# The queues of four engines tied to the order of the source, in a decoder block on one core

## The chip, the cores and the metric

The kernel runs on one core of one Trainium2 chip. The metric is the device time of one execution, in microseconds (us), as the median of several executions; less is better. The engines are named as the profile names them: PE (TensorE, matmuls and transposes; PEld are its weight loads), DVE (VectorE), ACT (ScalarE), POOL (GpSimd) and SP (SyncE, which issues most DMAs). Each engine works through a queue of its own, in the order in which the program was written out for it; between engines, semaphores hold an instruction back until what it reads or overwrites is ready.

## The reference

One layer of a decoder: a gated short convolution and stick-breaking attention run on the same normalised input, are merged by sigmoid gates and projected; then a gated MLP with a causal convolution between its up-projection and its gelu. 1024 tokens and 16 meta tokens, width 1024, 16 heads of 64, MLP width 2816, all in fp32:

```python
h = xn @ w_in
b_c, c_c, h_c, q, k, v, g_conv, g_attn = jnp.split(h, list(splits), axis=-1)
y_conv = b_c * causal_dwconv(c_c * h_c, conv_w_mix)
branch_conv = y_conv @ w_proj_conv
...
z = jnp.einsum("bqhd,bkhd->bhqk", qb, kb) * scale
log_beta = jax.nn.log_sigmoid(z)
log_fail = jnp.where(causal, log_beta - z, 0.0)
survive = lax.cumsum(log_fail, axis=3, reverse=True) - log_fail
a = jnp.where(causal, jnp.exp(log_beta + survive), 0.0)
...
merged = sigmoid(g_conv + b_gate[0]) * branch_conv + sigmoid(g_attn + b_gate[1]) * branch_attn
mixed = merged @ w_out
...
u, g = jnp.split(xn @ w_up_gate, 2, axis=-1)
u = causal_dwconv(u, conv_w_ffn)
return (jax.nn.gelu(u) * g) @ w_down
```

Around both parts stand RMS norms before and after, and the residual is added.

## The kernel before

**Precision.** Each fp32 operand of a matmul is split into a high and a low part (`split`, L64): ACT casts the high one (L65), and DVE or POOL subtracts it from the source for the low one (L66). A product then takes three matmuls: high by high, high by low, low by high.

**Stages**, by the clock of the profile:

- 0 to 80: inputs, norms, the transposed input xnT, and the first operands.
- 80 to 410: 14 *early pairs*, two column blocks of `w_in` each, for the convolution (c, h, b) and for gates. A pair is done by one level of Strassen's scheme (`strassen`): seven products in place of eight, for each of two halves of the tokens (260 columns). The seven operands S1, S2, A12 and so on are sums of blocks of the raw weights, made one step at a time by the generator `weight_ops` for the pair that comes next, into a ring of eight slots; the steps are called between the products. In each half, ACT copies the first three banks into `snap_e` (L600, L603, L606); later products add onto the same banks, so they wait for these copies. `done_ch` puts the convolution's steps on a list `todo`, whose entries are run one after each product: POOL's product c * h (L640), ACT's scaling (L643), DVE's two multiply-adds (L645 to L647).
- 410 to 1025: attention for eight pairs of heads, a period of about 70 us each. `stage1` makes the scores z on PE, ACT a sigmoid `fl` (L359), DVE a scan over it (L366). `stage2` transposes the scanned blocks (L394, PE), ACT casts the high part `ah` (L398), DVE makes the low part `al` (L401), PE multiplies both by the values (L384, L385), and ACT and DVE move the result out (L421, L422). In between run matmuls of the q, k and v projections (L138 to L140), with their evacuations `qh`, `ql` (L237, L238, L232), `kk` (L252, L256) and `vv` (L287, L288).
- 1025 to 1260: gates and the two branch projections. Rows that were written to DRAM are loaded again and split (`yT`, `oT`); gates leave PSUM through ACT (L332).
- 1260 to 1420: the out-projection by blocks of tokens, each with a norm (`post_block`, L1026 to L1059, which ends in the normalised `xv` and its transpose), and the first operands of the FFN (`op_split`, `x_t1` and so on).
- 1420 to 1833: the FFN's up-projection, 22 pairs of column blocks by the same Strassen scheme. Even pairs make u, in two halves of 258 and 256 columns; odd pairs make the gate, 512 columns wide. `products` (L1149 and after) has three copies into `snap` (L1169, L1172, L1175) at the same places, and `prep_pair` makes the operands of the next pair, a step after each product (a gate pair) or after every second one (a u pair), into a ring of eight slots. Between a u pair and its gate pair stands `conv_gelu` (L1333): for each of two blocks the convolution (`conv3`: ACT L204, DVE L205 and L206) and the Gelu (ACT L1337).
- 1833 to 2086: the down-projection, the last norm and the output.

**What sets the order.** The source writes the work out in one sequence, with generators that interleave the stages by hand. The framework then schedules it: in each engine's queue an instruction may be placed ahead of one that the source has earlier, where the framework's own estimate has it ready first. The order in the source is thus a wish, and the program's order the scheduler's. Of the instructions behind the first 80 us, 833 of PE's 12566 stand elsewhere than in the source (by at most 39 places), 1011 of DVE's 1691 (by up to 88), and on ACT and POOL 307 and 77 neighbours stand the other way round. The queue of SP and the DMAs are scheduled in the same way.

The loop of the FFN, for the place of `conv_gelu`:

```python
        if gate:
            conv_gelu(p)
            sets = [products(i, 1, 512, bank, evac_g(p))]
...
        for si, st in enumerate(sets):
            for k, _ in enumerate(st):
                if gate or (7 * si + k) % 2:
                    next(prep, None)
```

Of the kernel before, what the change touches and what calls it, by code (L numbers as in the profile page):

```python
# [33 lines left out]
def block_kernel(ctx, tc, x, meta_tokens, g_pre_mix, w_in, channels, w_proj_conv,  # L34
                 w_proj_attn, w_out, g_post_mix, g_pre_ffn, w_up_gate, w_down,
                 g_post_ffn, out):
    nc = tc.nc
# [409 lines left out]
    dense = Dense(ps_mm0, items)  # L447
# [94 lines left out]
    for i in range(2):  # L542
        next(tops_gen)
        start_chunk(i, 9)
    dense.i, dense.total = 2, 48

    RING1 = ["ap", "ap", "ap", "ap", "wlo", "whi", "wlo", "whi"]
    ring1_at = [2]
# [182 lines left out]
    for i in range(len(early_pairs)):  # L731
        last = i + 1 == len(early_pairs)
# [104 lines left out]
                cur, credit = cur + 1, 0.0  # L837


    at_ctx.close()  # L840
    slots_abc = ctx.enter_context(ExitStack())
    slotA = slots_abc.enter_context(pool("slotA", 1, "right"))
# [584 lines left out]
    for gi, fbs in enumerate(groups):  # L1427
        last = gi == len(groups) - 1
# [13 lines left out]
        for tb in range(8):  # L1442
# [23 lines left out]
            if last:  # L1466
# [3 lines left out]
                for hf in range(2):  # L1470
# [2 lines left out]
                                                   op0=ALU.mult, op1=ALU.add)  # L1473
                    (nc.sync if hf else nc.scalar).dma_start(out[tb * P:(tb + 1) * P, c], a[:, c])


# [1 line left out]
_OUTS = [((1024, 1024), "float32")]  # L1478
# [53 lines left out]
```

## Time and profile before

| | |
|---|---|
| median of 3 executions | 2082.77 us (2081.93 to 2088.43) |
| the profiled execution | 2088.08 us, of which its span 2086.3 us |
| PE clock granted, mean | 0.981 of full speed |
| instructions | 31469 |
| largest groups by busy time | matmuls L138, L139, L140 (291.5, 280.3, 279.9 us) and the FFN's L1160, L1162, L1164 (171.1, 169.0, 168.8 us) |
| DVE's largest group | the scans L366, 195.7 us |

The stage table in the prediction has, for each stretch of the span, the busy microseconds of each engine with the number of instructions, then the granted clock of PE as a share of full speed, the busy share of the DMA engines, and GB/s. A row of a timeline is: start, duration, engine, line, operation, output and inputs with their shapes; a bracket behind it has the idle time of that engine just before and what ended it. A row of the waits is: the engine and what waited, what it waited for, and then the sum, the count and the longest one, in us.

### The profile page before, as it was taken

The page shows a single profiled execution, that of the slowest core. Times are in us where ns is not written, and L with a number is a line of the kernel's source. Part 1 is how long each engine was busy: PE and PEld are TensorE (multiplying, and loading weights), DVE is VectorE, ACT ScalarE, POOL GpSimd, SP SyncE. Part 2 cuts the span into 40 slices and gives each one's busy share as a digit, 9 for nine tenths or more (in the row PEclk, how much of TensorE's full clock was granted, in tenths as well). Part 3 has the DMA queues.
Part 4 walks back from the last instruction along what each step waited for, and adds up shares of the span by engine and source line. Part 5 has one row for each costly group of instructions (what it writes and reads, how often), then busy time and mean ns, then how long its engine had stood idle before and what let it go on. Part 6 is the DMA issues. An engine that isn't in the chain of part 4 may idle for free.

```text
span 2086.3 us, 31469 instructions
## 1 busy us (share of the span) xinstructions
PE 1970.3 (94%) x12564; PEld 1842.9 (88%) x12564; DVE 1109.3 (53%) x1689; ACT 838.7 (40%) x1709; POOL 815.9 (39%) x644
## 2 busy tenths in 40 slices
PE   6889999999999999999999989979999999999997
PEld 6889999998999899889999989978899899878886
DVE  6733443247777777776342114785444444445546
ACT  6433333435555555555441212354334434412122
POOL 2644544422221222122122561225656555555353
PEclk9999999999999999999999999999999999999999
DMA  3212221310100010002374574313222121253323
GB/s 133 87 55 62 70 67 47 109 44 21 41 31 21 31 41 31 21 31 61 85 239 172 168 201 129 101 56 101 71 92 81 61 102 67 76 182 101 101 81 131
DMA packets 56175, 177.60 MB, mean 85 GB/s; under 512 B 12872, under 2 KB 12872, under 8 KB 56028
## 3 DMA queue, kind: packets, MB, share of 16 engines
q1 hardware_dynamic: 52704, 165.09, 24.7%
q10 hardware_dynamic: 3324, 10.50, 1.6%
q8 instruction: 98, 1.61, 0.3%
q14 instruction: 49, 0.40, 0.1%
HBM read 131.36 MB, written 44.21 MB: 84 GB/s over the span
## 4 chain that ended last, share of the span: by engine, by line
PE 36%; DMA 6%; DVE 5%; POOL 3%; ACT 2%; issue 1%; ACTq 0%; SPq 0%; DVEq 0%; POOLq 0%
PE st L1160 6%; PE st L1164 5%; PE st L1162 5%; PE st L1454 3%; PE st L1452 3%; PE st L1453 3%; PE mm L138 2%; PE mm L139 2%; PE mm L140 2%; POOL a_op L66 1%; DMA raw<-in_w_up_gate_dram 1%; DMA ld<-y_d 1%; DVE xr L69 1%; PE po L1007 1%; PE po L1009 1%
## 5 line engine op out<-in xcount | busy, mean ns | idle before, releaser
L122 POOL TENSOR_TENSOR wlo<-raw,whi 128x256 fp32r<-128x256 f32 x208 | 172.4, 859 | 331.0 <-ACT whi L119 307.1
L138 PE MATMUL mm<-xnT,whi 128*128 128x342 f32 (+1 forms) x864 | 291.5, 338 | 7.7 <-ACT gt L332 3.6
L140 PE MATMUL mm<-xnT,wlo 128*128 128x342 f32 (+1 forms) x864 | 279.9, 324 | 3.6 <-POOL wlo L122 3.6
L139 PE MATMUL mm<-xnT,whi 128*128 128x342 f32 (+1 forms) x864 | 280.3, 324 | 0.1
L66 POOL TENSOR_TENSOR a_op<-raw,a_op 128x512 fp32r<-128x512 f32 (+1 forms) x136 | 191.9, 1425 | 91.6 <-ACT a_op L65 87.3
L366 DVE TENSOR_TENSOR_SCAN fl<-fl,upper 114x128 f32<-114x128 f32 (+2 forms) x144 | 195.7, 1379 | 28.2 <-ACT fl L359 26.9
L69 DVE TENSOR_TENSOR raw<-raw 128x512 f32<-128x512 f32 x72 | 72.1, 1001 | 210.3 <-POOL a_op L66 106.3
L1160 PE MATMUL st<-opT,a_op 128*128 128x258 f32 (+2 forms) x528 | 171.1, 324 | 6.6 <-ACT snap L1175 3.8
L138 PEld LDWEIGHTS mm<-xnT,whi 128*128 128x128 f32 x864 | 165.6, 192 | 11.7 <-ACT gt L332 4.2
L1162 PE MATMUL st<-opT,a_op 128*128 128x258 f32 (+2 forms) x528 | 169.0, 320 | 1.3 <-DVE v L76 0.9
L140 PEld LDWEIGHTS mm<-xnT,wlo 128*128 128x128 f32 x864 | 165.3, 191 | 4.2 <-POOL wlo L122 4.2
L1164 PE MATMUL st<-opT,a_op 128*128 128x258 f32 (+2 forms) x528 | 168.8, 320 | 0.0
L139 PEld LDWEIGHTS mm<-xnT,whi 128*128 128x128 f32 x864 | 165.8, 192 | 1.8 <-DVE xnT L66 0.7
L590 PE MATMUL st<-tT,s_op 128*128 128x260 f32 x448 | 130.3, 291 | 20.6 <-ACT snap_e L600 16.3
L65 ACT CAST a_op<-raw 128x512 fp32r<-128x512 f32 (+1 forms) x136 | 85.1, 634 | 159.8 <-DMA raw<-in_w_up_gate_dram 56.6
L1459 DVE TENSOR_TENSOR acc<-acc,st 128x512 f32<-128x512 f32 x144 | 98.4, 687 | 91.1 <-PE st L1454 91.1
L398 ACT CAST ah<-tp 114x342 fp32r<-114x342 f32 (+3 forms) x288 | 109.0, 400 | 91.9 <-PE tp L394 87.2
L401 DVE TENSOR_TENSOR al<-tp,ah 114x342 fp32r<-114x342 f32 (+3 forms) x288 | 118.1, 449 | 35.1 <-ACT ah L398 32.6
L66 POOL TENSOR_TENSOR s_op<-raw,s_op 128x512 fp32r<-128x512 f32 x84 | 119.6, 1437 | 40.9 <-ACT s_op L65 30.2
L359 ACT ACTIVATE fl<-z 114x348 f32<-114x348 f32 (+10 forms) x240 | 109.9, 464 | 61.4 <-PE z L358 60.8
L594 PE MATMUL st<-tT,s_op 128*128 128x260 f32 x448 | 129.0, 288 | 0.0
L592 PE MATMUL st<-tT,s_op 128*128 128x260 f32 x448 | 129.0, 288 | 0.0
(200 smaller groups left out, 5556.9 us busy)
## 6 DMA issues: line engine op xcount, KB each, us to landing
raw<-in_w_in_dram SPq DMA_DIRECT2D x64, 512.0 KB, 3.4
raw<-in_w_up_gate_dram SPq DMA_DIRECT2D x44, 512.0 KB, 3.5
act_d<-owork SPq DMA_DIRECT2D x22, 512.0 KB, 4.3
araw<-act_d SPq DMA_DIRECT2D x22, 512.0 KB
raw<-in_w_down_dram SPq DMA_DIRECT2D x22, 512.0 KB, 3.2
y_d<-su SPq DMA_DIRECT2D x8, 513.0 KB
o_d<-ot SPq DMA_DIRECT2D x8, 513.0 KB
ld<-y_d SPq DMA_DIRECT2D x8, 513.0 KB, 5.2
```

The lines of the kernel that those rows point to most:

```text
L66: (lo_engine or nc.vector).tensor_tensor(lo, src, hi.bitcast(F32), op=ALU.subtract)
L122: nc.gpsimd.tensor_tensor(lo[:, c], raw[:, c], hi[:, c].bitcast(F32), op=ALU.subtract)
L138: nc.tensor.matmul(ps, wh, xh, start=(kb == 0), stop=False)
L139: nc.tensor.matmul(ps, wh, xl, start=False, stop=False)
L140: nc.tensor.matmul(ps, wl, xh, start=False, stop=(kb == KB - 1))
L366: nc.vector.tensor_tensor_scan(fl[:, ::-1], fl[:, ::-1], upper[:, NT - nk:][:, ::-1], 1.0, op0=ALU.mult, op1=ALU.max)
L590: nc.tensor.matmul(ps, wt[:, 0, k], xh, start=start and kb == 0, stop=False, skip_group_check=True)
L592: nc.tensor.matmul(ps, wt[:, 0, k], xl, start=False, stop=False, skip_group_check=True)
L594: nc.tensor.matmul(ps, wt[:, 1, k], xh, start=False, stop=stop and kb == 3, skip_group_check=True)
L1160: nc.tensor.matmul(ps, wt[:, 0, k], xh, start=start and kb == 0, stop=False, skip_group_check=True)
L1162: nc.tensor.matmul(ps, wt[:, 0, k], xl, start=False, stop=False, skip_group_check=True)
L1164: nc.tensor.matmul(ps, wt[:, 1, k], xh, start=False, stop=stop and kb == 3, skip_group_check=True)
```

## The change

Two edits. Before the attention stage's buffers are given back, a generator of weight operands (`dense`) is run on by one step. And at the end of the program a function walks over all instructions that came after the preamble, in the order of the source, and ties each one of PE, ACT, DVE and POOL, other than DMA issues, to the one before it on the same engine. These ties make no semaphore wait; they only keep the scheduler from putting a later instruction first. SP and the DMAs are left free.

```diff
@@ -543,6 +543,7 @@
         start_chunk(i, 9)
     dense.i, dense.total = 2, 48
+    first = len(nc.cur_bb.bb.instructions)
 
@@ -837,6 +838,8 @@
+    if dense.gen is not None:
+        dense.until(dense.i + 1)
     at_ctx.close()
@@ -1473,6 +1476,22 @@
+    in_program_order(tc, nc, first)
+
+
+def in_program_order(tc, nc, first, engines=("PE", "Activation", "DVE", "Pool")):
+    last = {}
+    for ins in list(nc.cur_bb.bb.instructions)[first:]:
+        name = ins.engine.name
+        if name not in engines or "DMA" in type(ins).__name__.upper():
+            continue
+        if name in last:
+            tc.add_manual_dep(ins, last[name].name,
+                              mybir.DependencyInfo(mybir.DependencyClass.NoSync,
+                                                   mybir.DependencyReason.DATA),
+                              reason="program order")
+        last[name] = ins
```

Lines behind L546 move down by one, those behind L840 by three: L600 becomes L601, L1169 becomes L1172, L1337 becomes L1340.

**ACT around a gate pair of the FFN.** The rows of the program before, from the end of a u pair on (a_op and raw are operands of the next pair, owork the convolution's tiles, st a bank, snap its copy):

```order
L204 ACTIVATE owork<-owork,par_ffn 128x1024
L1213 COPY owork<-st 128x255
L204 ACTIVATE owork<-owork,par_ffn 128x1024
L65 CAST a_op<-raw 128x512
L1169 COPY snap<-st 128x512
L1337 ACTIVATE owork<-owork 128x1024
L65 CAST a_op<-tmp_s 128x512
L1172 COPY snap<-st 128x512
L1337 ACTIVATE owork<-owork 128x1024
```

The same place after the change:

```order
L1216 COPY owork<-st 128x255
L65 CAST a_op<-raw 128x512
L204 ACTIVATE owork<-owork,par_ffn 128x1024
L1340 ACTIVATE owork<-owork 128x1024
L204 ACTIVATE owork<-owork,par_ffn 128x1024
L1340 ACTIVATE owork<-owork 128x1024
L1172 COPY snap<-st 128x512
L65 CAST a_op<-raw 128x512
```

The first bank's copy stood between the second L204 and the first Gelu, and now stands behind both Gelus; the second L204 now stands behind the first Gelu.

**ACT around a pair of the early stage** that follows on a finished c and h (s_op are operands of the next pair; su the tiles of the result). Before:

```order
L704 COPY su_1139<-st_1246 128x260
L643 ACTIVATE su_1138<-su_919,par_66 128x1026
L643 ACTIVATE su_1139<-su_920,par_66 128x1026
L600 COPY snap_e_592<-st_1359 128x260
L65 CAST s_op_1388<-raw_1353 128x512
L603 COPY snap_e_592<-st_1360 128x260
L606 COPY snap_e_592<-st_1359 128x260
L704 COPY su_1358<-st_1359 128x260
L65 CAST s_op_1420<-tmp_e_591 128x512
L600 COPY snap_e_592<-st_1468 128x260
L65 CAST s_op_1451<-raw_1353 128x512
```

After:

```order
L601 COPY snap_e_592<-st_1359 128x260
L604 COPY snap_e_592<-st_1360 128x260
L65 CAST s_op_1388<-raw_1353 128x512
L607 COPY snap_e_592<-st_1359 128x260
L65 CAST s_op_1420<-tmp_e_591 128x512
L65 CAST s_op_1451<-raw_1353 128x512
L644 ACTIVATE su_1138<-su_919,par_66 128x1026
L705 COPY su_1358<-st_1359 128x260
L601 COPY snap_e_592<-st_1468 128x260
L65 CAST s_op_1483<-raw_1353 128x512
L644 ACTIVATE su_1139<-su_920,par_66 128x1026
L604 COPY snap_e_592<-st_1469 128x260
```

The two scalings (L643, then L644) stood ahead of the pair's first snap and now stand behind the three of its first half; the casts of S1 and S2 (s_op_1420 and s_op_1451) stood around the first snap of the second half (from st_1468), and now both stand ahead of it.

**DVE in the attention stage**, at the block of scans near 630 us (fl are scanned, qh and ql evacuate the q projection, al is the low part that PE waits for). Before:

```order
L366 SCALAR_TENSOR_TENSOR fl_6406<-fl_6406,upper_4035 114x242
L366 SCALAR_TENSOR_TENSOR fl_6415<-fl_6415,upper_4035 114x356
L366 SCALAR_TENSOR_TENSOR fl_6424<-fl_6424,upper_4035 114x470
L366 SCALAR_TENSOR_TENSOR fl_6433<-fl_6433,upper_4035 114x584
L366 SCALAR_TENSOR_TENSOR fl_6449<-fl_6449,upper_4035 114x698
L238 CAST qh_6273<-mm_6394 64x342
L401 TENSOR_TENSOR al_6490<-tp_6485,ah_6489 128x342
L401 TENSOR_TENSOR al_6501<-tp_6496,ah_6500 114x342
L238 CAST qh_6274<-mm_6394 64x342
L232 TENSOR_TENSOR ql_6275<-mm_6394,qh_6273 64x342
```

After:

```order
L366 SCALAR_TENSOR_TENSOR fl_6264<-fl_6264,upper_4035 114x1040
L366 SCALAR_TENSOR_TENSOR fl_6400<-fl_6400,upper_4035 114x128
L366 SCALAR_TENSOR_TENSOR fl_6406<-fl_6406,upper_4035 114x242
L366 SCALAR_TENSOR_TENSOR fl_6415<-fl_6415,upper_4035 114x356
L366 SCALAR_TENSOR_TENSOR fl_6424<-fl_6424,upper_4035 114x470
L366 SCALAR_TENSOR_TENSOR fl_6433<-fl_6433,upper_4035 114x584
L238 CAST qh_6273<-mm_6394 64x342
L238 CAST qh_6274<-mm_6394 64x342
L232 TENSOR_TENSOR ql_6275<-mm_6394,qh_6273 64x342
L232 TENSOR_TENSOR ql_6276<-mm_6394,qh_6274 64x342
L422 TENSOR_TENSOR ot_6237<-av_6311,ot_6237 64x342
L401 TENSOR_TENSOR al_6490<-tp_6485,ah_6489 128x342
```

The scan of 1040 columns stood some dozen rows higher and is now at the head of the block; both qh and both ql now stand ahead of the first al, and the scan of 698 (fl_6449) behind the row shown last.

## The prediction

> **What bounds the kernel now.** I read the page first, then the busy times by stage, then what TensorE (PE) waited for, and then the stretches in which the order of a queue decides.
>
> ```profile
> PE 1970.3 (94%) x12564; PEld 1842.9 (88%) x12564; DVE 1109.3 (53%) x1689; ACT 838.7 (40%) x1709; POOL 815.9 (39%) x644
> ```
>
> PE is busy for 94% of the span of 2086.3 us: 116 us of the whole program are without a matmul, so an order that only removes waits can't gain more than that and the time at half clock. An order that makes PE wait has no such limit. The stages:
>
> ```profile
> core 0: us, PE busy (x) PEld busy (x) DVE busy (x) ACT busy (x) POOL busy (x), PEclk, DMA share, GB/s
> ...
> 410.00:1025.00 615.00, 587.09 (x3918) 558.55 (x3916) 433.26 (x659) 332.67 (x772) 135.43 (x148) 1.00 0.11 36
> ...
> 1420.00:1833.00 413.00, 410.31 (x2566) 367.10 (x2564) 183.68 (x222) 170.00 (x293) 237.93 (x176) 1.00 0.24 82
> ```
>
> The reader is to see two things. In the FFN's up-projection (1420 to 1833) PE idles 2.7 us of 413: nothing is left to gain there, and any wait that the new order makes is a loss in full. In the attention stage (410 to 1025) DVE is busy 433 of 615 us, so its queue has the least room. What PE waits for:
>
> ```profile
> PE st L590 <- ACT snap_e L600: 16.3, 4, 4.1
> PE tp L394 <- DVE al L401: 13.6, 21, 1.8
> ...
> PE av L385 <- DVE al L401: 8.0, 11, 1.0
> PE tp L1046 <- DVE xv L1039: 6.8, 1, 6.8
> ...
> PE mm L138 <- ACT gt L332: 5.2, 3, 3.3
> ```
>
> All of them are waits for the two engines whose queues the change rewrites. PE itself hardly moves (833 of its 12566 instructions change place, by at most 39), and DMAs are not ordered. So the question is, place by place, what stands ahead of the instruction that PE waits for.
>
> **Gate pairs of the FFN: the largest term.** Around the first product of such a pair the profile has
>
> ```profile
> 1531.04 0.40 PE L1160 MATMUL st<-opB,a_op 128*128 128x512 f32 x1
> ...
> 1536.62 0.40 PE L1160 MATMUL st<-opT,a_op 128*128 128x512 f32 x1
> ```
>
> ```profile
> 1530.35 1.15 ACT L204 ACTIVATE owork<-owork,par_ffn 128x1024 f32<-128x1024 f32 x1
> 1531.41 0.37 ACT L1213 COPY owork<-st 128x255 f32<-128x255 f32 x1
> ...
> 1534.53 0.58 ACT L1169 COPY snap<-st 128x512 f32<-128x512 f32 x1
> 1535.00 1.06 ACT L1337 ACTIVATE owork<-owork 128x1024 f32<-128x1024 f32 x1
> ```
>
> ```profile
> 1534.32 1.28 DVE L205 SCALAR_TENSOR_TENSOR owork<-owork,par_ffn 128x1024 f32<-128x1024 f32 x1
> ```
>
> The first row opens the first of the pair's products of 12 matmuls, the second row the third one, 5.58 us later (2.79 a product). The third adds onto the bank of the first, so it needs the copy L1169 of that bank, which now is made at 1534.53, ahead of the Gelus. In the new order ACT has: cast, copy of the last u bank, cast of A22', L204, Gelu, L204, Gelu, and only then that copy. The chain can't start before the last u copy ends (1531.78): A22' cast 0.53 until the next may start; first L204 1.15; L205 (1.28 by its row) and L206, of the same shape, on DVE, 2.56; Gelu 1.06, of which the next L204 waits 1.0; L204 1.15; DVE 2.56; Gelu 1.06, of which 0.95 counts; copy 0.58. That is 10.5 us, to 1542.3, and with some 0.07 us for each of five hand-overs between engines to 1542.6. PE wants it at 1536.62: it waits 6.0 us. Nothing behind may pass: PE's own order is now fixed too, and the products run one after the other. The bounds: 5.0 if the A22' cast, the hand-overs and one overlap cost nothing; 7.0 if the DVE operations take 1.5 us, as some of them do.
>
> Half clock comes on top. The row for it is the same sort of gap in the early stage:
>
> ```profile
> 146.00:150.00 4.00, 0.21 (x2) 0.00 (x1) 3.45 (x1) 1.57 (x3) 2.80 (x2) 0.80 0.40 131
> 150.00:157.00 7.00, 6.70 (x37) 6.71 (x38) 6.04 (x7) 1.42 (x4) 1.54 (x1) 0.63 0.00 0
> ```
>
> These are the columns of the stage table for one of the four waits for snap_e (4.1 each): PE does nothing from 146.2 to 150.3. A granted clock of 0.63 over the 7 us behind it is 5.2 us at half speed (7 x 0.37 / 0.5), of which 4.9 lie after the wait: PE loses 2.45 us after a gap of 4.1. In the gap itself 0.80 over 4 us is 1.6 us at half speed, so the clock fell 2.4 us into it. For a gap of 6 I take 2.0, between 1.6 (the same 6.8 us at half speed in all, 3.6 of them inside the gap) and 2.45. There are 11 gate pairs: 11 x (6.0 + 2.0) = **+88 us**, bounds 11 x 6.6 = 73 and 11 x 9.5 = 104. [...]
>
> **u pairs of the FFN and the early pairs: the operand ring.** In both loops the cast of S2' (L65) needs the slot of an operand that the second half's second product still reads, and the new order puts it ahead of the first snap of that half. In the early stage the rows are now
>
> ```profile
> 136.26 0.62 ACT L65 CAST s_op<-raw 128x512 fp32r<-128x512 f32 x1 [0.55 <-PE st L594]
> 136.79 0.37 ACT L603 COPY snap_e<-st 128x260 f32<-128x260 f32 x1
> ...
> 148.83 1.15 ACT L643 ACTIVATE su<-su,par 128x1026 f32<-128x1026 f32 x1 [2.43 <-POOL su L640]
> 149.89 0.36 ACT L600 COPY snap_e<-st 128x260 f32<-128x260 f32 x1
> ```
>
> The cast at 136.26 waited for the end of PE's second product; the first snap had been made before it. After the change the snap stands behind: cast 0.53, a bank copy 0.3, snap 0.37, and about 0.2 of hand-overs give a PE wait of 1.4 us in each pair, taken as too short for the half clock. u pairs: 10 x 1.4 = **+14 us** (10, or 31 with 1.7 of half clock each). Early pairs: 13 x 1.4 = 18; in four of them L643 (1.15) stands between as well and makes the wait 2.5, with 1.7 of half clock: 4 x (1.1 + 1.7) = 11; later raw loads 13 x 0.25 = 3; together 32. Against that the four waits of 4.08 go, since L643 (148.83), which waits for POOL's L640, then stands behind the snaps: 4 x (4.08 + 2.45) = 26. Sum **+6 us** (-15 to +28).
>
> **Attention: DVE's queue.** The last term of size, and the least certain. Rows of one period (there are eight, of 70 us):
>
> ```profile
> 616.38 0.57 ACT L359 ACTIVATE fl<-z 114x462 f32<-114x462 f32 x1
> ...
> 617.13 2.08 DVE L366 TENSOR_TENSOR_SCAN fl<-fl,upper 114x926 f32<-114x926 f32 x1
> ...
> 623.16 2.31 DVE L366 TENSOR_TENSOR_SCAN fl<-fl,upper 114x1040 f32<-114x1040 f32 x1
> ...
> 634.39 1.58 DVE L366 TENSOR_TENSOR_SCAN fl<-fl,upper 114x698 f32<-114x698 f32 x1
> ...
> 637.51 0.52 DVE L238 CAST qh<-mm 64x342 fp32r<-64x342 f32 x1
> 638.04 1.04 DVE L232 TENSOR_TENSOR ql<-mm,qh 64x342 fp32r<-64x342 f32 x2
> ```
>
> First place: the scan of 926 gets its input at 616.95 (616.38 + 0.57), and L422 and L288 run ahead of it today; in the new order it is ahead of them, DVE idles until its input is there, and the vv of L288 comes after the scan and two qh, 2.08 + 2 x 0.52 later, while PE waits for it to free a bank. I take 1.5 us (0 to 3.1). Second place: ahead of al (which starts on DVE between the row of 634.39 and that of 637.51) come the scan of 1040 (2.31), the second qh (0.52) and both ql (1.04), and the scan of 698 (1.58) goes behind: 2.3 us more, so that PE's wait there, 0.65 as a mean now (13.6 / 21), becomes about 3, and a gap of that length costs about 1.7 at half clock (estimated from the 2.45 of a gap of 4.1). Per period 1.5 + 2.3 + 1.7 = 5.5, and eight periods give **+44 us**. Bounds: 0, if the waits for al of now (13.6 + 8.0 us in all) go in exchange; 12 per period or +96, if DVE's lag adds up over its three bursts of scans.
>
> **The rest.** In the transition from attention to the projections ACT's casts of loaded rows stand ahead of L332 and wait for their DMA; the wait of 3.3 us may become 6: **+3** (-3 to +10). From 1260 to 1420 the wait of 6.8 for xv goes, because post_block stands ahead of the operand splits on DVE; ACT's squares and Gelus then hold up the snaps of the first pairs: **+5** (-15 to +20). The down-projection keeps its order but for one swap: 0.
>
> **Sum.** 88 + 14 + 6 + 44 + 3 + 5 = +160 us. The profiled execution took 2088.08 us (its span and 1.8 around it); 2248 against it, and 2243 against the median, which lies 5.3 lower.
>
> **Rivals.**
> - Attention is a wash (the al waits of now pay for the new ones): 2083 + 88 + 14 + 14 = 2199. For it: each engine has idle time there, DVE 30%. Against: al stands behind more work by rows. Chance 0.20.
> - DVE becomes the bound in attention: +96 in place of +44, 2295. For it: scans are 2.3 us long and come in bursts, and an in-order lag also delays what ACT waits for. Chance 0.13.
> - The gate chain is mostly covered: if the copy of a u bank and the first L204 run ahead by more than I think, or PE holds work back, 2.5 us instead of 8 per gate pair: 2243 - 60 = 2183; with attention at zero, 2140. Chance 0.09.
> - Faster: the source's order is itself a pipeline that fits. Place: the first bank's copy in a gate pair; price: the 88 us go; it decides if the chain from L204 to the second Gelu ends within the 5.6 us of two products. Then the early waits (26), the al waits (22) and xv (7) are gained and only the ring is lost (46): 2083 - 9, or 2060 if the ring is half covered. Against it stand the durations, which add to 10.5. Chance 0.07.
> - The change does nothing: the queues of ACT and DVE would have to come out as before, and they don't. A chance of 0.03 for gains and losses that cancel.
>
> **Numbers.** The forecast has 0.48. Slower by over 0.3% (6 us, about what a measurement of this kernel tells from no change) 0.48 + 0.20 + 0.13 + 0.09 = 0.90; within 0.03; faster 0.07. The range leaves out the last two cases alone: it goes from 2125 (the gate chain covered and attention at zero, 2140, with the ring and the early stage at their low ends) to 2310 (DVE as the bound, 2295, with the stage from 1260 at its high end).
>
> **What would show it.** In the profile after, PE should wait 11 times about 6 us for the copy that is L1172 there, and DVE's second Gelu input should end last before it; L590's (then L591's) waits of 4.1 should be gone, with some 13 short ones for snaps in their place; waits for al should grow and their number fall; and the stage from 1420 should last about 100 us longer. Wrong would be the sum if the third product of a gate pair starts without a wait, or if PE's idle time in attention is 28 us as now.

## The result, and the profile after

| | before | after |
|---|---|---|
| median | 2082.35 us (2078.64 to 2088.43, 4 executions) | 2328.82 us (2322.13 to 2335.77, 4 executions) |
| ratio | | 1.118 (95% interval 1.1137 to 1.1225) |
| profiled execution, span | 2086.3 us | 2329.2 us |
| PE clock granted, mean | 0.981 | 0.952 |

The change makes the kernel 246 us slower. The direction is the forecast one; the time lies 19 us above the upper end of the range.

The first page of the profile after, its row of busy times:

```profile
PE 2032.2 (87%) x12564; PEld 1890.8 (81%) x12564; DVE 1085.5 (47%) x1689; ACT 835.0 (36%) x1709; POOL 811.8 (35%) x644
```

The same 12564 matmuls keep PE busy 62 us longer (2032.2 against 1970.3), since more of them run at half clock (a matmul of 512 columns takes 0.63 us at a granted clock of 0.50, from 1630.9 to 1633.0, and 0.40 at full clock behind that), and PE's idle time grows from 116 to 297 us, by 181. These two make the 243 us by which the span grew. Where it is, by stage (each stage cut at its first and last matmuls, so that both kernels are cut at the same instruction; columns as in the prediction):

```profile
core 0: us, PE busy (x) PEld busy (x) DVE busy (x) ACT busy (x) POOL busy (x), PEclk, DMA share, GB/s
105.40:462.50 357.10, 307.01 (x2356) 300.07 (x2355) 110.31 (x160) 104.16 (x218) 159.40 (x108) 0.95 0.18 59
462.50:1124.00 661.50, 595.30 (x3859) 566.31 (x3859) 445.38 (x655) 332.89 (x769) 137.38 (x143) 0.97 0.10 33
1124.00:1350.20 226.20, 219.37 (x1375) 218.52 (x1374) 53.16 (x112) 54.83 (x103) 92.82 (x106) 0.98 0.63 197
1350.20:1462.10 111.90, 108.98 (x707) 108.27 (x706) 65.06 (x153) 43.48 (x111) 24.17 (x13) 0.98 0.38 114
1462.10:2075.30 613.20, 483.41 (x2789) 426.20 (x2789) 204.67 (x271) 195.42 (x337) 243.71 (x184) 0.91 0.18 59
2075.30:2329.20 253.90, 241.03 (x1057) 198.01 (x1055) 135.36 (x226) 53.28 (x81) 117.61 (x57) 0.99 0.36 120
```

| stage | before | after | difference | forecast |
|---|---|---|---|---|
| to the first early pair | 98.4 | 105.4 | +7 | 0 |
| early pairs | 316.7 | 357.1 | +40 | +6 |
| attention | 607.5 | 661.5 | +54 | +44 |
| gates and projections | 237.2 | 226.2 | -11 | +3 |
| out-projection and FFN up to its end | 572.0 | 725.1 | +153 | +107 |
| down-projection | 254.5 | 253.9 | -1 | 0 |

What PE waited for in the kernel after (sum, times, longest):

```profile
PE st L1163 <- ACT snap L1172: 94.5, 23, 11.8
PE tp L394 <- DVE al L401: 36.0, 22, 3.8
PE st L591 <- DVE su L707: 23.0, 12, 3.4
PE st L591 <- ACT snap_e L601: 20.5, 13, 2.3
PE st L1163 <- DVE owork L1218: 18.2, 9, 2.6
PE st L1163 <- ACT snap L1178: 15.6, 11, 3.5
PE av L385 <- DVE al L401: 12.3, 7, 1.9
```

Rows one, two and four are waits that the prediction named. Row one holds the eleven gate pairs (9.7 us in the first, 5.5 in each of the ten others), ten waits of 1.25 us in the u pairs, and two of 5.2 and 11.8 us in the first u pair. The four waits of 4.1 us for snap_e of before are gone, as forecast, and the 13 short ones of row four are near the forecast's sum for them (13 x 1.4 + 4 x 1.1 = 22.6). Rows three, five and six were not named.

The gate pair of the FFN, on ACT and then on PE, in the kernel after:

```profile
1620.03 1.15 ACT L204 ACTIVATE owork<-owork,par_ffn 128x1024 f32<-128x1024 f32 x1
1623.93 1.06 ACT L1340 ACTIVATE owork<-owork 128x1024 f32<-128x1024 f32 x1 [2.76 <-DVE owork L206]
1624.90 1.13 ACT L204 ACTIVATE owork<-owork,par_ffn 128x1024 f32<-128x1024 f32 x1
1628.70 1.06 ACT L1340 ACTIVATE owork<-owork 128x1024 f32<-128x1024 f32 x1 [2.67 <-DVE owork L206]
1629.66 0.57 ACT L1172 COPY snap<-st 128x512 f32<-128x512 f32 x1
```

```profile
1630.28 0.79 PE L1163 MATMUL st<-opT,a_op 128*128 128x512 f32 x1 [5.52 <-ACT snap L1172]
```

ACT idles 2.7 us ahead of each Gelu, with the copy that PE needs behind it in the queue, and PE waits 5.5 us: the chain of the prediction, step by step.

The start of the u pair that follows, on DVE and on PE:

```profile
1655.70 0.69 DVE L1135 TENSOR_TENSOR tmp_s<-raw 128x512 f32<-128x512 f32 x1 [9.19 <-DMA raw<-in_w_up_gate_dram]
1656.31 0.42 DVE L1218 TENSOR_TENSOR owork<-st,snap 128x258 f32<-128x258 f32 x1
1656.65 0.68 DVE L69 TENSOR_TENSOR raw<-raw 128x512 f32<-128x512 f32 x1
1657.43 0.69 DVE L69 TENSOR_TENSOR raw<-tmp_s,raw 128x512 f32<-128x512 f32 x1
1658.04 0.75 DVE L1218 TENSOR_TENSOR owork<-st,snap 128x258 f32<-128x258 f32 x2
```

```profile
1652.76 0.39 PE L1163 MATMUL st<-opT,a_op 128*128 128x258 f32 x1 [1.22 <-ACT snap L1178]
1658.52 0.39 PE L1163 MATMUL st<-opT,a_op 128*128 128x258 f32 x1 [2.63 <-DVE owork L1218]
```

DVE had nothing to do for 9.2 us, but the three additions L1218, whose banks PE waits for, stand behind tmp_s (two of them behind two subtractions L69 as well), and tmp_s waits for the DMA of the next pair's weights. This is the wait that the prediction missed.

### The profile page after: what moved, and what is told of

Read it like the earlier page. It is cut to its first block, busy times and chain, and to the rows that moved or that the text cites. A ratio compares the mean times of both kernels' runs of the same rounds, so it can differ in the third digit from the quotient of the medians.

```text
span 2329.2 us, 31516 instructions
## 1 busy us (share of the span) xinstructions
PE 2032.2 (87%) x12564; PEld 1890.8 (81%) x12564; DVE 1085.5 (47%) x1689; ACT 835.0 (36%) x1709; POOL 811.8 (35%) x644
## 5 line engine op out<-in xcount | busy, mean ns | idle before, releaser
L122 POOL TENSOR_TENSOR wlo<-raw,whi 128x256 fp32r<-128x256 f32 x208 | 165.4, 826 | 489.5 <-ACT whi L119 449.9
L138 PE MATMUL mm<-xnT,whi 128*128 128x342 f32 (+1 forms) x864 | 295.5, 343 | 17.2 <-ACT gt L332 9.6
L1163 PE MATMUL st<-opT,a_op 128*128 128x258 f32 (+2 forms) x528 | 188.0, 356 | 129.6 <-ACT snap L1172 94.5
L139 PE MATMUL mm<-xnT,whi 128*128 128x342 f32 (+1 forms) x864 | 283.2, 328 | 0.1
L66 POOL TENSOR_TENSOR a_op<-raw,a_op 128x512 fp32r<-128x512 f32 (+1 forms) x136 | 185.3, 1369 | 280.6 <-ACT a_op L65 277.0
L1163 PEld LDWEIGHTS st<-opT,a_op 128*128 128x128 f32 x528 | 108.7, 206 | 150.4 <-ACT snap L1172 101.6
L138 PEld LDWEIGHTS mm<-xnT,whi 128*128 128x128 f32 x864 | 168.4, 195 | 20.9 <-ACT gt L332 10.1
L69 DVE TENSOR_TENSOR raw<-raw 128x512 f32<-128x512 f32 x72 | 58.3, 810 | 267.0 <-POOL s_op L66 133.7
L1165 PE MATMUL st<-opT,a_op 128*128 128x258 f32 (+2 forms) x528 | 180.7, 342 | 0.2 <-DVE opT L66 0.2
L1167 PE MATMUL st<-opT,a_op 128*128 128x258 f32 (+2 forms) x528 | 179.5, 340 | 0.0
L591 PE MATMUL st<-tT,s_op 128*128 128x260 f32 x448 | 134.2, 300 | 50.1 <-DVE su L707 23.0
L139 PEld LDWEIGHTS mm<-xnT,whi 128*128 128x128 f32 x864 | 169.0, 196 | 1.9 <-DVE xnT L66 0.7
L394 PE MATMUL tp<-ident,fl 114*114 114x114 f32 (+1 forms) x720 | 118.2, 270 | 43.4 <-DVE al L401 36.0
L394 PEld LDWEIGHTS tp<-ident,fl 114*114 114x114 f32 (+1 forms) x720 | 88.9, 140 | 56.4 <-DVE al L401 42.6
```

The lines of the kernel that those rows point to most:

```text
L66: (lo_engine or nc.vector).tensor_tensor(lo, src, hi.bitcast(F32), op=ALU.subtract)
L122: nc.gpsimd.tensor_tensor(lo[:, c], raw[:, c], hi[:, c].bitcast(F32), op=ALU.subtract)
L138: nc.tensor.matmul(ps, wh, xh, start=(kb == 0), stop=False)
L139: nc.tensor.matmul(ps, wh, xl, start=False, stop=False)
L394: nc.tensor.transpose(tp[:n, QB * j:QB * (j + 1)], blocks[j][0][:, k0:k0 + n], ident[:QB, :QB])
L591: nc.tensor.matmul(ps, wt[:, 0, k], xh, start=start and kb == 0, stop=False, skip_group_check=True)
```

## The experiments

All of them edit the changed kernel, but for the two that say otherwise. `free` is a set of instructions that `in_program_order` passes over, so that the scheduler may place them as before. Single executions are compared with the kernel before on the same chip (2078.6 us for the first four, 2075.5 for the next four, 2078.9 for the three behind e9).

### One engine at a time

```diff
-    in_program_order(tc, nc, first)
+    in_program_order(tc, nc, first, ("Activation",))     # e1
+    in_program_order(tc, nc, first, ("DVE",))            # e2
+    in_program_order(tc, nc, first, ("PE", "Pool"))      # e3
+    in_program_order(tc, nc, first, ("PE",))             # e5
+    in_program_order(tc, nc, first, ("Activation", "DVE", "Pool"))   # e8
```

> Only ScalarE's instructions are tied to the order of the source. Theory A (each loss belongs to the queue in which the late instruction stands): the wait for the first bank's copy in a gate pair of the FFN is made by ScalarE's queue alone, so 11 x (5.5 us + about 2 at half clock) = 83 stay, the ring waits of 1.25 us stay in the FFN and the early pairs (23 x 1.25 = 29), and the four early waits of 4.1 with their half clock (26) are gone: 2083 + 83 + 29 - 26 = 2169, between 2150 and 2200. Theory B (TensorE's fixed order is what makes the waits cost): under 2100. Theory C (the losses need all the queues tied at once, since the scheduler arranges the free engines around one tied queue): under 2120.

> Only VectorE is tied. Theory A: attention loses its 54 us, the early waits for su (23 us and half clock) and the FFN's waits for owork at the start of a u pair (18 us and half clock) come too, while the four early waits of 4.1 of before stay: 2083 + 54 + 30 to 50, so 2150 to 2190, with no wait for the first copy of a gate pair. Theory B: under 2100. Theory C: attention under +20, and 2120 at most.

> Only TensorE and GpSimd are tied. Theory A: within 10 us of the kernel before, 2075 to 2095, with the four waits of 4.1 as before. Theory B: most of the loss is here, 2200 or more.

> Only TensorE is tied. With TensorE and GpSimd tied the attention stage grew by 25 us (607 to 632) and the FFN by 20. Theory D (the matmuls that the scheduler had pulled ahead cover the waits for al): the 25 us of attention are TensorE's and stay, 2100 to 2112. Rival (GpSimd's order made them, through the low parts of the weights): attention within 6 us of before, under 2092.

> ScalarE, VectorE and GpSimd tied, TensorE left to the scheduler. Theory D: a good part of attention's 54 us goes, since TensorE can be arranged around the later al: attention 625 to 645, and 2295 to 2315 in all, the FFN's waits as in the changed kernel. Rival (the three queues alone make the loss, wherever TensorE's matmuls stand): attention 655 to 662 and 2320 to 2335.

| tied | time | early | attention | FFN |
|---|---|---|---|---|
| none (before) | 2082.4 | 317 | 607 | 461 |
| ACT | 2193.2 | 326 | 621 | 565 |
| DVE | 2108.4 | 335 | 614 | 468 |
| PE | 2107.0 | 316 | 635 | 462 |
| PE and POOL | 2121.7 | 321 | 632 | 482 |
| ACT, DVE, POOL | 2233.1 | 337 | 611 | 588 |
| all (the change) | 2328.8 | 357 | 661 | 613 |

e1 fell into the range of theory A, and nearly all its loss is the FFN's, where ACT's queue alone makes a wait for the snap. But its total agrees better than its parts: ten gate pairs wait 3.8 to 4.0 us each, not 5.5; the ring's waits of 1.25 us don't come; and the early stage grew by 10 us, where the theory had it 10 shorter (13 x 1.25 - 26), since the waits for snap_e went and PE waits 19.6 us for su L707 in their place. e2 and e3 did not fall into theory A's range; e2 came out as theory C said, which e1 refutes for ACT. e2 was to show attention's loss as DVE's own: attention grew by 6 us, with DVE's queue in the order of the change. e3 was to cost nothing, and cost 43 us. The window of attention in e2, e5 and e8, one row of each:

```profile
430.30:1043.90 613.60, 584.03 (x3859) 555.28 (x3859) 439.97 (x655) 328.80 (x768) 143.41 (x139) 0.99 0.10 35
```

```profile
412.80:1047.50 634.70, 580.40 (x3860) 552.61 (x3858) 433.02 (x655) 329.88 (x769) 128.65 (x139) 0.99 0.10 34
```

```profile
440.70:1052.10 611.40, 580.69 (x3860) 553.51 (x3859) 442.13 (x655) 331.31 (x769) 139.35 (x143) 0.99 0.10 36
```

The first column after the window is its length. With PE alone tied attention takes 634.7, with everything but PE tied 611.4: of the 54 us, 50 need PE's ties. PE's ties alone cost 27, those of the other three alone 4, and 23 come only with both; which of the three engines adds these 23, no run shows. PE's free place was worth 96 us in the whole kernel with the other three tied (2328.8 - 2233.1), more than either theory gave it: 50 in attention, 20 in the early stage and 25 in the FFN, where ten gate pairs wait 3.7 us each in e8. So PE's order has a share in what the other stages lose, too.

### Which of PE's matmuls: e12

```diff
+                    n0 = len(nc.cur_bb.bb.instructions)
                     nc.tensor.matmul(ps, wh, xh, start=(kb == 0), stop=False)
                     nc.tensor.matmul(ps, wh, xl, start=False, stop=False)
                     nc.tensor.matmul(ps, wl, xh, start=False, stop=(kb == KB - 1))
+                    if attention:
+                        free.update(k.name for k in list(nc.cur_bb.bb.instructions)[n0:])
```

> All four engines tied, but TensorE's projection matmuls in the attention stage (L138 to L140) left to the scheduler; transposes, scores and value products stay tied. With TensorE free as a whole the stage took 611 us, with all tied 661. If what covers the waits for al is that projection matmuls may stand between a value product with ah and the one with al: 610 to 622, and 2280 to 2290 in all. Rival (the place of the transposes and the value products among themselves covers them): 645 or more, 2312 or more.

Measured: 2279.3 us, attention

```profile
461.00:1073.30 612.30, 579.26 (x3859) 554.93 (x3859) 443.32 (x655) 332.66 (x769) 139.43 (x143) 0.99 0.11 36
```

and the waits of tp for al fall from 36.0 to 15.0 us in that stage. So it is the projection matmuls. In the program before and in the changed one PE's queue reads, at one of these places:

```
before                                    after
av_6203<-ah_6208,vv_5340 128x342          av_6203<-ah_6208,vv_5340 128x342
mm_6194<-xnT_86,whi_5884 128x342          av_6203<-al_6209,vv_5340 128x342
mm_6194<-xnT_86,whi_5884 128x342          av_6203<-ah_6214,vv_5340 128x228
mm_6194<-xnT_86,wlo_5885 128x342          av_6203<-al_6215,vv_5340 128x228
mm_6194<-xnT_86,whi_5884 128x342          mm_6194<-xnT_86,whi_5884 128x342
av_6203<-al_6209,vv_5340 128x342          mm_6194<-xnT_86,whi_5884 128x342
```

The scheduler had put projection matmuls (four here, one to seven at other places of this period) between the product with ah and the one with al. Moves of so few places are what hid DVE's lateness.

### The FFN: e4, e6, e10

e4 leaves conv_gelu to the scheduler, e6 also prep_pair (by lines like those of e11 below); e10 ties everything and loads the weights of a pair one pair earlier, into a tile that is free by then:

```diff
     def conv_gelu(p):
+        n0 = len(nc.cur_bb.bb.instructions)                                    # e4, e6
...
+        free.update(i.name for i in list(nc.cur_bb.bb.instructions)[n0:])      # e4, e6
```

```diff
-                raw = wpool.tile([P, D], F32, name="raw", tag="raw")
+                raw = (spare[0][:, k * D:(k + 1) * D] if even
+                       else wpool.tile([P, D], F32, name="raw", tag="raw"))    # e10
...
-        load_pair(i + 1)
+        if i == 0:
+            load_pair(1)
+        load_pair(i + 2)                                                       # e10
```

> All four engines tied, but the instructions of conv_gelu (both L204, L205, L206 and both Gelus of a pair) left to the scheduler. Theory A: the 11 waits of a gate pair for its first copy go, about 60 us and some 20 of half clock with the first, longer ones, all else stays: 2329 - 85 = 2244, between 2225 and 2260. Rival: the time comes back as a later wait, since the Gelus still have to be done before the gate's first evacuation: 2300 or more.

> As the run with conv_gelu left to the scheduler (2247, its FFN part 535 us against 461 before), and with all of prep_pair (the operands of the next FFN pair: the loads of raw, tmp_s, the subtractions, the casts) left to it too. If the rest of the FFN's loss is operand work that stands in order ahead of what TensorE waits for (the ring's casts ahead of the snaps, and tmp_s and the first cast, which wait for a DMA, ahead of the owork additions and the third snap): the FFN part falls to 465 to 485, 2177 to 2197 in all. Rival (only the ring's 1.25 us a pair is operand work, the other waits come from the products' own order): the FFN part stays over 515, 2228 or more.

> All four engines tied, the FFN's raw weights loaded one pair earlier into a second set of buffers (a tile of the transposed input that is free by then), so that tmp_s and the first cast of a pair don't wait for their DMA. If the waits at the start of a u pair (for snap L1178, about 1.2 us, and for owork L1218, 1.2 to 2.6 us) come from tmp_s and the cast, which stand ahead of them in order and wait for the DMA: they go, with about 1.5 us of half clock a pair, and the FFN part falls from 613 us to 565 to 580, 2329 - 40 = 2289. Rival (the operand steps are late for the ring's slots or for GpSimd, not for the DMA): 600 us or more, 2315 or more.

Measured: 2247.2, 2181.8 and 2283.2 us; the FFN's row of e4, of e6, and of e10:

```profile
1456.30:1991.20 534.90, 466.36 (x2790) 415.75 (x2789) 223.57 (x272) 197.00 (x338) 255.71 (x184) 0.95 0.20 68
```

```profile
1458.50:1925.80 467.30, 445.10 (x2790) 400.63 (x2789) 222.52 (x276) 199.85 (x338) 251.44 (x182) 0.97 0.22 76
```

```profile
1461.70:2027.60 565.90, 470.49 (x2791) 417.77 (x2790) 213.40 (x272) 196.16 (x338) 248.74 (x184) 0.92 0.19 64
```

All three came out as the theory that operand work and Gelus stand ahead of the snaps said. conv_gelu is worth 613 - 535 = 78 us, the operand steps another 535 - 467 = 68, and what is left of the FFN's loss is 6. e10 takes 47 us away with every tie in place. From 1500 us to the end of its FFN PE waits for this alone:

```profile
PE st L1172 <- ACT snap L1181: 77.5, 21, 9.7
```

The waits for owork (18.2) and for the third snap (15.6) are gone: they were waits for a DMA, passed on by two queues. The rest of the operand steps' 68 is some 21 us; the ring's ten waits of 1.25 us would be 12.6 of them, and no run took these apart from the others.

### The early stage: e7, e11, e9

e7 frees the convolution's steps, e11 the operand steps. e9 is the kernel before, with only L643 tied, behind the newest snap:

```diff
-                    todo.pop(0)()
+                    run_free(todo.pop(0))                                      # e7
...
+            n0 = len(nc.cur_bb.bb.instructions)
+            done = next(st, st) is st
+            free.update(k.name for k in list(nc.cur_bb.bb.instructions)[n0:])  # e11
```

```diff
+                    def scaled(src=src, dst=dst, cb=cb):
+                        nc.scalar.activation(dst, src[:, 2:2 + NQ], AF.Copy, scale=w_mix(2, cb))
+                        behind(last_ins(), newest["snap"])                     # e9
```

> All four engines tied, but the convolution's steps of the early stage (todo: GpSimd's products L641, ScalarE's L644, VectorE's L648 and the closing products) left to the scheduler. If the new waits for su L707 (1.9 and 3.4 us in each convolution pair) and the 1 us on top of the ring's 1.25 come from those steps in the queues: the early stage falls from 357 us to about 325, 2329 - 32 = 2297, if the waits of 4.1 of before don't come back; with them 2320. Rival (the waits for su come from operand work that waits for its DMA ahead of them): 345 to 357, and 2317 or more.

> All four engines tied, but the operand steps of the early stage (weight_ops: tmp_e, subtractions, casts and low parts) left to the scheduler; the convolution's steps stay tied. With the latter freed the stage stayed at 350 us. If its loss is operand work ahead of the snaps and of the su additions: the early stage falls from 357 to 320 to 332, and 2329 - 31 = 2298 in all. Rival (it takes both, operand and convolution steps, or TensorE's order): 345 or more, 2315 or more.

> The kernel before with one kind of tie only: the eight scalings L643 of the early stage, which wait for GpSimd, are tied behind the newest snap on ScalarE's queue, everything else is left to the scheduler. If the four waits of 4.1 us with 2.45 of half clock each come from L643 standing ahead of the snaps: they go, and nothing replaces them, 2083 - 26 = 2057, ratio 0.985 to 0.99. Rival (TensorE is held up again some products later, by su or the ring): 2070 to 2083.

Measured: e7 2320.9 us, its early stage 349.5 (the rival's number); e11 2271.5 us, its early stage

```profile
104.40:408.50 304.10, 288.86 (x2356) 286.76 (x2355) 107.30 (x160) 105.96 (x217) 154.75 (x107) 0.98 0.22 69
```

which is 53 us less than with all tied, more than forecast, and 12.6 less than in the kernel before. So with all else in order the stage's loss is operand work, as in the FFN. e9: 2076.9 us (10 executions) against 2078.2, ratio 0.9998 (0.9988 to 1.0007), where 2057 was expected and the rival had 2070 to 2083. Its waits:

```profile
PE st L600 <- DVE su L721: 20.0, 10, 3.0
```

The four waits of 4.1 for a snap are gone, and eight of 2.0 and 2.2 for su have come in their place. DVE ahead of the first of them:

```profile
149.16 0.85 DVE L566 TENSOR_TENSOR tmp_e<-raw 128x512 f32<-128x512 f32 x1 [7.36 <-DMA raw<-in_w_in_dram]
150.10 0.69 DVE L69 TENSOR_TENSOR raw<-raw 128x512 f32<-128x512 f32 x1
150.89 0.69 DVE L69 TENSOR_TENSOR raw<-tmp_e,raw 128x512 f32<-128x512 f32 x1
151.50 1.28 DVE L662 SCALAR_TENSOR_TENSOR su<-su,par 128x1026 f32<-128x1026 f32 x1
152.70 0.75 DVE L721 TENSOR_TENSOR su<-st,snap_e 128x260 f32<-128x260 f32 x2
```

The sum tmp_e, two subtractions of the operand steps and a multiply-add of the convolution stand on DVE ahead of the additions L721 that free PE's banks, and tmp_e waited 7.4 us for its DMA. To move L643 moved the wait. Whether a load one pair earlier would have brought the 26 us, as it brought 47 in the FFN, was not run.

### All four groups, and a version that beats both: e13, e14

e13 frees conv_gelu, prep_pair, weight_ops and the projection matmuls of attention at once. e14 is the kernel before with the ties in the loop of the early pairs alone, weight_ops left free:

```diff
+    first = len(nc.cur_bb.bb.instructions)
     for i in range(len(early_pairs)):
...
     for fn in todo:
         fn()
+    in_program_order(tc, nc, first, free=free)
```

> All four engines tied, with the four groups left to the scheduler together: conv_gelu and prep_pair in the FFN, weight_ops in the early stage, TensorE's projection matmuls in attention. Each alone gave back 78 + 68, 53 and 49 us. If these four account for the whole loss and don't work on one another: the stages of the single runs add to 104 + 304 + 612 + 226 + 110 + 467 + 254 = 2078, 2080 with what lies around the span, a ratio of 0.995 to 1.004. Rival (part of the loss stays when each group's cover is taken by another, or comes from what is still tied): 2100 or more.

> The kernel before with ties in the early pairs' loop alone (all four engines, without the operand steps weight_ops). In the run with weight_ops free that stage took 304 us, against 316.6 in the kernel before. If that is the loop's own gain, and nothing behind it pays: 2083 - 12 = 2071, ratio 0.993 to 0.996. Rival (the gain was a shift of work into the preamble, which was 6 us longer there, or out of the loop): no change, 0.998 to 1.003.

Measured: e13 2085.4 us (10 executions), ratio 1.0023 (1.0012 to 1.0034); e14 2067.5 us (4 executions), ratio 0.9931 (0.9908 to 0.9953). With the four groups free the change costs 0.2%: they account for the loss, and their single amounts (78 + 68 + 53 + 49 = 248) add up to it. e14 is the fastest version: its early stage takes 303.5 us and the stages behind it are near those of before. Of the 13 us that this stage gains, 4.7 are waits (15.9 us idle against 20.6) and 8.6 are matmuls that are busy for less time, at a mean clock of 0.99 against 0.95: its four longest waits behind the first pair are 2.25 us, where the kernel before has four of 4.1.

## Why the prediction was right in direction and too small

The table's forecasts add to 160 us and the span grew by 243. Of the 82 us that the rows differ by, 46 lie in the row of the FFN, 34 in the early pairs, 10 in attention and 7 ahead of the early pairs; the gates and projections and the down-projection take 15 back. Two steps failed above all: the walk of a u pair's start, which was not made, and the early pairs' additions on DVE, for which nothing was put down.

**Gate pairs, +88: right.** The wait was put at 6.0 us and is 5.5 in ten of the eleven; half clock was put at 2.0 and costs 2.2 behind these ten as a mean (last section). With conv_gelu freed 78 us go.

**The ring, +14 in the FFN: right in itself, and the smaller part of its kind.** Its wait was put at 1.4 us and is 1.25. But the operand steps as a whole cost 68 us. The step that failed is the walk of a u pair's start: it was not made, and later loads of raw were counted in the early stage alone, at 0.25 us a pair. In order, tmp_s and the first cast stand ahead of L1218 and of the third snap, so that a late DMA is handed on to PE; e10 shows this to be 47 us.

**Early pairs, +6: wrong, +40.** The ring's waits came as forecast (1.25 in a plain pair, 2.3 in a convolution pair, against 1.4 and 2.5), and the four waits of 4.1 went as forecast. The forecast counted half clock for the longer of these waits alone, at 1.7 us each, which no row showed: of the four waits of 2.3, two were followed by it, with 1.5 us lost behind each, and none of the nine of 1.25 was. What failed is that the credit of 26 us for them was taken in full, with nothing put down for what is late next once the snaps are on time: in the kernel after PE waits 23.0 us for DVE's additions (su L707) and 6.5 us for the third snaps (snap_e L607). e9 and e1 show the same exchange with fewer ties. That the operand steps are the cause is shown by e11 (53 us), and that the convolution's steps alone are not by e7 (8 us); in e8, with PE free, the stage loses 20 us less.

**Attention, +44: nearly the right size, from half of the cause.** The scans do stand ahead of al, the wait that was to grow to about 3 us is 3.3 in six periods and 3.8 in a seventh, and each of these is followed by 3.4 us at half clock, 1.7 lost, as estimated. But with DVE in this very order and PE free the stage loses 6 us (e2), and 4 with ACT and POOL tied too (e8). The sentence that failed is the one that set PE aside: it "hardly moves". PE's ties cost 27 us by themselves (e5) and are needed for 50 of the 54. Moves of a few places are enough, since a few projection matmuls between two value products cover a wait; e12 gives 49 of the 54 us back by freeing these alone. So that +44 lies so near +54 is in part luck: the working puts down to DVE's order alone what needs both.

**The rest.** The 7 us ahead of the early stage were not seen: two new waits of 4.5 and 5.1 us there, for L332 and L119. They come with ACT, DVE and POOL tied and PE free as well (4.8 and 4.0 us in e8), while with one engine tied alone none there is over 3.7; no run took them further apart. The gates and projections took 230 to 237 us in three profiles in which that stage is ordered as before (before, e9, e14), and 225 to 227 in those with all or nearly all tied, so only some 3 to 12 us of gain can be there, and no run looked for its cause. The +5 from 1260 on is near: the wait of 6.8 for xv is gone, and the first u pair waits 5.2 and 11.8 us for its first copies, which stand on ACT behind a norm and behind casts of the FFN's token operands; the waits at this place were 11.5 us before (6.8, 1.7, 1.7 and 1.3). The down-projection is unchanged, as forecast.

**The rivals.** The one that takes DVE as the bound in attention had the nearest total (2295), and is refuted: DVE is busy 445 of 661 us, and e8 has the same DVE work in 611. That attention is a wash is refuted for the change by its +54, and is nearly what e8 shows where PE is free. The case of a gate chain that is covered is refuted by the 5.5 us. That the source's order is itself a fitting pipeline is refuted for the whole kernel; with the operand steps left out it holds for the early loop, by 0.7% (e14). The 2060 given there for a half covered ring is a slip: 2083 - 55 + 23 is 2051.

## What to carry to other kernels

Before an order is fixed, list for each queue the instructions that wait longest (for a DMA, for another engine's chain), and look at what stands behind each of them: in order, that wait is handed to whoever needs the next instruction (here DVE's 9.2 us for a DMA were followed by 2.6 us of PE's for owork). Don't set the bottleneck engine aside because few of its instructions move: a handful of independent matmuls between two dependent ones can be all the cover there is (here one to seven of them, and 49 of attention's 54 us in e12). And test ties in groups: here fixing one loop, with the work that waits for loads left free, gained 0.7%, where fixing everything lost 12%.

## What the runs showed of the hardware that was not expected

How long PE ran at half clock behind a gap did not follow from the gap's length alone. Two gate pairs, each with a wait of 5.5 us (the first row of each two is the wait, the second what follows; columns of the window table):

```profile
1624.80:1630.20 5.40, 0.00 (x0) 0.00 (x0) 3.86 (x4) 2.73 (x5) 0.00 (x0) 0.96 0.00 0
1630.20:1637.20 7.00, 6.92 (x24) 5.59 (x25) 1.77 (x1) 3.17 (x7) 3.83 (x3) 0.79 0.00 0
...
1677.40:1682.90 5.50, 0.02 (x1) 0.00 (x0) 3.87 (x4) 2.82 (x5) 0.00 (x0) 0.82 0.00 0
1682.90:1690.00 7.10, 7.07 (x21) 5.60 (x22) 1.77 (x1) 3.12 (x6) 3.14 (x3) 0.66 0.00 1
```

In the first the clock fell only at the end of the wait, and a mean of 0.79 over 7 us is 2.9 us at half speed, 1.5 us lost. In the second it fell 3.5 us into the wait (0.82 over 5.5 us is 2.0 at half speed), and 0.66 over 7.1 us is 4.8 us at half speed, 2.4 lost. Over the ten pairs with this wait the trace's clock records give 2.2 us lost as a mean, from 1.4 to 2.8: the forecast's 2.0 had the right size. In the early stage before, a wait of 4.1 had the clock fall after some 2.2 us and lost 2.45.

Shorter waits go either way. These are two of the waits for owork, the first with a wait of 1.2 us ahead of it in the same row:

```profile
1651.50:1660.00 8.50, 4.65 (x37) 4.41 (x37) 2.99 (x6) 0.89 (x2) 1.28 (x1) 1.00 0.24 95
...
1766.40:1772.40 6.00, 5.97 (x36) 5.79 (x36) 0.31 (x1) 0.62 (x1) 0.56 (x1) 0.73 0.00 0
```

The first row holds a wait of 2.6 us and no half clock at all; the second lies behind a wait of 2.5 us, and 0.73 over 6 us is 3.2 us at half speed, 1.6 lost. Of the six such waits between 2.2 and 2.7 us, four brought half clock. In the early stage all eight waits of 2.0 and 2.2 us of e9 brought it, but only one of the four of 2.25 us in e14, which by these two profiles is most of why e14 gained and e9 did not. The mean granted clock of the whole execution is 0.984 in e9 and 0.988 in e14, against 0.985 and 0.983 in the runs of the kernel before beside them. What decides whether a wait of this length brings half clock, no run shows. Every spell at half clock in the FFN's up-projection after the change lasts 3.4, 6.8 or 10.2 us by the trace's clock records. Over the whole execution a mean of 0.952 is 224 us at half speed (0.048 x 2329.2 / 0.5), against 79 before (0.019 x 2086.3 / 0.5).
